# Gate and up of the first column group by turns, finer first splits, one place for split tiles in all phases, norm transposes apart

## The chip, the cores and the metric

The kernel runs on one core of one Trainium2 chip. The metric is the device time of one execution in microseconds (us). A core has a matrix engine (PE, with its weight loads PEld), a vector engine (DVE), a scalar engine (ACT), a third elementwise engine (POOL), and a queue engine that issues the weight loads from memory (SP). The granted clock of PE is written as a share of its full speed.

## The reference, cut to what matters

A decoder layer on x of 256 rows by 2048 columns, all in float32: a SwiGLU half-step (ffn1), a mixer of attention and gated linear attention, a cross-attention into 256 memory rows, and a second SwiGLU half-step (ffn2).

```python
def swiglu(h, w_gate, w_up, w_down):
    return (jax.nn.silu(h @ w_gate) * (h @ w_up)) @ w_down
...
        x = x + 0.5 * swiglu(rms_norm(x, ffn1_norm[l]), ffn1_w_gate[l], ffn1_w_up[l], ffn1_w_down[l])
        x = x + hybrid_mixer(rms_norm(x, mix_norm[l]), pos, w_in[l], attn_q_norm[l], attn_k_norm[l],
                             gla_w_gate2[l], gla_b_gate2[l], gla_out_norm[l], w_out[l])
        x = x + cross_attention(rms_norm(x, xattn_norm[l]), rms_norm(mem, mem_norm[l]),
                                xattn_w_q[l], xattn_w_k[l], xattn_w_v[l],
                                xattn_q_norm[l], xattn_k_norm[l], xattn_w_o[l])
        x = x + 0.5 * swiglu(rms_norm(x, ffn2_norm[l]), ffn2_w_gate[l], ffn2_w_up[l], ffn2_w_down[l])
```

w_gate and w_up have 2048 x 5632 elements, w_down 5632 x 2048.

## The kernel before, in words

**Precision and tiles.** Every float32 product is made of three passes in a reduced format: a weight tile `raw` of 1 MiB (128 partitions, four k-steps of 512 columns) is split into `wh` (a cast on ACT) and `wl = raw - wh` (a subtraction on DVE), both recorded at L145 in `split`, and PE adds wh·xh, wl·xh and wh·xl. One such tile against the 256 rows is a group of 24 matmuls of 512 columns. Activations stand transposed and split as xTh and xTl (a pair for each of four chunks of 512 columns), hTh and hTl, and sh and sl (sums for the Strassen products).

**Phases.** `open_phase` and `close_phase` stack a pool for the half-step phases (half1, half2) and for the middle phase between. `wh` and `wl` have three places each in a half-step, four smaller ones in the middle phase; raw tiles come from `wp` (three places) and in a half-step, by turns, from the phase's own three (`load`, L130 and below). `in_turn` keeps the weight loads, the casts and the subtractions each in the program's order.

**A half-step** (`ffn`, L372 and below) takes 11 column groups of gate and up in the parts 0 to 3, 4 to 7, 8 to 10, and after each part the products with w_down. The first column group is a plain projection (`proj`): gate's four k-groups, then up's four. All others, and w_down, go through `strassen` (L228 and below): six products P1 to P6 of 12 matmuls each on two PSUM tiles x and y, then whole groups of 24 with one more product (on `ral`, with the sum accumulated by DMA) between. P1 takes the left tile `ral`; DVE then adds the right tile to it (L237), which is split again for P2, added to again and split again for P3. ACT evicts c0l (L254) and ys (L260), DVE makes c0r = ys - x (L264), which must be done before P5 writes x again, and c1r (L269). L219 and L184 are the matmuls in a Strassen, L175 to L177 those of a plain projection.

**Turning h and x.** h of a column group is transposed on PE (L383) two steps of the program after it is made (`later(2, ...)`, counted by `tick`), and hTh is copied by ACT (L302) and hTl subtracted by DVE (L303). At the end of ffn1 and at the end of the cross-attention `norm_chunk` squares a finished chunk of x on ACT (L332) and transposes it one step later (L343); DVE multiplies by the gain (xg, L345), ACT and DVE split (L348, L349).

**The order of work.** A scheduler puts each engine's instructions in a row by priority; `tc.high_priority(WPRI)` (200) lifts the splits of weights, evictions and accumulations. The split of h (L301 to L303) is not lifted. At the start, three raw tiles of gate and three tiles `xr` of x transposed are requested ahead of everything (L115 and below); `first` multiplies xr by the gain (POOL, or ACT for the first four pieces) and splits it. `load_x` fetches x in rows and squares it.

## Time and profile before

| what | value |
| --- | --- |
| median of three runs | 1917.93 us (1915.93 to 1919.88) |
| the profiled execution: its time | 1920.29 us |
| its span in the trace | 1918.5 us |
| PE busy | 1890.5 us, 99% |
| DVE busy | 1459.3 us, 76% |
| ACT busy | 1080.1 us, 56% |
| POOL busy | 125.7 us, 7% |
| mean granted clock | 0.995 |
| bytes moved by DMA | 453.90 MB, 237 GB/s in the mean |

A row of the timeline gives the start in us from the span's start, the busy time, the engine, the line of the kernel, the operation with what it writes and reads, the count of instructions put together in the row, and in square brackets the idle time of the engine ahead of it with what released it. Where several instructions stand in one row the busy time is that of all of them. The windows give busy time of each engine in a stretch, the mean granted clock, the share of the DMA engines and the bytes per second.

### The profile page before, as it was taken

How to read it: one execution, taken by the hardware profiler on the slowest of the kernel's cores; microseconds unless marked ns; L12 is line 12 of the kernel's file. 1: busy time of each engine (PE TensorE's matmuls, PEld its weight loads, DVE VectorE, ACT ScalarE, POOL GpSimd, SP SyncE). 2: the span in 40 equal slices, each digit the busy share in tenths (PEclk: the TensorE clock that was granted, in tenths of full speed). 3: DMA queues.
4: the chain of work that ended last, by engine and by line, in shares of the span. 5: the costliest groups of instructions: out<-in, count | busy, mean ns of one | idle time of the engine just before them, and what ended most of it. 6: DMA issues, size and time to landing. Idle time of an engine off the chain costs nothing.

```text
span 1918.5 us, 21566 instructions
## 1 busy us (share of the span) xinstructions
PE 1890.5 (99%) x8616; PEld 1563.4 (81%) x8616; DVE 1459.3 (76%) x1159; ACT 1080.1 (56%) x1028; POOL 125.7 (7%) x137
## 2 busy tenths in 40 slices
PE   8999999999999999999999999899999999999998
PEld 6888888888888778778888889788888888888876
DVE  7779887788888885446785555777888878888886
ACT  6556655555555556444676445555655556556553
POOL 2000000000000000002230000000000000000000
PEclk9999999999999999999999999899999999999999
DMA  9776787777877754445465554668768777787775
GB/s 376 274 244 225 241 301 280 275 240 241 277 246 274 250 157 174 169 158 194 174 221 200 195 193 157 254 198 293 231 230 285 259 275 272 246 284 233 242 253 171
DMA packets 68480, 453.90 MB, mean 237 GB/s; under 512 B 7675, under 2 KB 8827, under 8 KB 15004
## 3 DMA queue, kind: packets, MB, share of 16 engines
q1 hardware_dynamic: 56284, 370.74, 49.2%
q0 software_dynamic: 10944, 79.70, 18.5%
q10 hardware_dynamic: 1152, 2.10, 0.3%
q8 instruction: 67, 1.10, 0.2%
q14 instruction: 33, 0.27, 0.0%
HBM read 379.10 MB, written 6.29 MB: 201 GB/s over the span
## 4 chain that ended last, share of the span: by engine, by line
PE 93%; DVE 4%; issue 1%; ACT 1%; DMA 1%; POOL 0%; SPq 0%; DVEq 0%; POOLq 0%; ACTq 0%
PE acc L184 24%; PE x L219 17%; PE acc L176 9%; PE acc L177 9%; PE acc L175 9%; PE acc L219 9%; PE x L184 8%; PE y L219 4%; DVE wl L145 2%; ACT wh L145 1%; PE tp L383 1%; DVE raw L237 1%; DMA xr<-in_xT_dram 0%; DMA raw<-raw 0%; PE tp L343 0%
## 5 line engine op out<-in xcount | busy, mean ns | idle before, releaser
L145 DVE TENSOR_TENSOR wl<-raw,wh 128x2048 fp32r<-128x2048 f32 (+2 forms) x523 | 1013.6, 1954 | 367.1 <-ACT wh L145 366.7
L145 ACT CAST wh<-raw 128x2048 fp32r<-128x2048 f32 (+2 forms) x523 | 852.2, 1640 | 621.3 <-DVE raw L237 182.2
L175 PE MATMUL acc<-wh,xTh 128*128 128x512 f32 x544 | 216.3, 399 | 9.0 <-ACT wh L145 8.8
L176 PE MATMUL acc<-wl,xTh 128*128 128x512 f32 x544 | 214.9, 395 | 4.6 <-DVE wl L145 4.6
L177 PE MATMUL acc<-wh,xTl 128*128 128x512 f32 x544 | 214.2, 394 | 0.0
L237 DVE TENSOR_TENSOR raw<-raw 128x2048 f32<-128x2048 f32 x64 | 146.5, 2290 | 1.7
L241 POOL DMA_DIRECT2D raw<-raw x64 | 55.0, 860 | 1201.2 <-ACT sg L420 473.8
L175 PEld LDWEIGHTS acc<-wh,xTh 128*128 128x128 f32 x544 | 103.1, 190 | 32.4 <-ACT wh L145 10.5
L176 PEld LDWEIGHTS acc<-wl,xTh 128*128 128x128 f32 x544 | 103.6, 190 | 28.0 <-DVE wl L145 6.9
L184 PE MATMUL acc<-wl,xTh 128*128 128x512 f32 x480 | 121.8, 389 | 0.0
L184 PE MATMUL acc<-wh,xTl 128*128 128x512 f32 x480 | 121.8, 389 | 0.0
L184 PE MATMUL acc<-wh,xTh 128*128 128x512 f32 x480 | 121.8, 389 | 0.0
L177 PEld LDWEIGHTS acc<-wh,xTl 128*128 128x128 f32 x544 | 103.6, 190 | 21.7
L184 PEld LDWEIGHTS acc<-wl,xTh 128*128 128x128 f32 x480 | 90.1, 188 | 18.7
L184 PEld LDWEIGHTS acc<-wh,xTh 128*128 128x128 f32 x480 | 90.1, 188 | 18.7
L184 PEld LDWEIGHTS acc<-wh,xTl 128*128 128x128 f32 x480 | 90.1, 188 | 18.7
L219 PE MATMUL x<-wh,sh 128*128 128x512 f32 x256 | 71.2, 400 | 3.3 <-ACT wh L145 1.9
L219 PE MATMUL x<-wh,sl 128*128 128x512 f32 x256 | 68.8, 390 | 0.0
L219 PE MATMUL x<-wl,sh 128*128 128x512 f32 x256 | 68.7, 390 | 0.0
L420 ACT ACTIVATE sg<-acc,r 128x512 f32<-128x512 f32 x24 | 16.3, 689 | 84.7 <-PE acc L184 84.7
L184 PE MATMUL acc<-wh,hTl 128*128 128x512 f32 x232 | 59.2, 390 | 2.4 <-DVE hTl L303 2.4
L184 PE MATMUL acc<-wh,hTh 128*128 128x512 f32 x232 | 59.2, 390 | 0.9 <-ACT wh L145 0.9
(339 smaller groups left out, 2828.3 us busy)
## 6 DMA issues: line engine op xcount, KB each, us to landing
raw<-in_ffn_w_up_dram SPq DMA_DIRECT2D x88, 1024.0 KB, 8.9
raw<-in_ffn_w_down_dram SPq DMA_DIRECT2D x88, 1024.0 KB, 7.6
raw<-in_ffn_w_gate_dram SPq DMA_DIRECT2D x85, 1024.0 KB, 7.8
raw<-raw POOLq DMA_DIRECT2D x64, 1024.0 KB, 6.9
raw<-in_w_in_dram SPq DMA_DIRECT2D x48, 1024.0 KB, 4.8
raw<-in_w_out_dram SPq DMA_DIRECT2D x16, 1024.0 KB, 4.8
sl<-ffn_sl POOLq DMA_DIRECT2D x4, 1024.0 KB, 9.4
sh<-ffn_sh POOLq DMA_DIRECT2D x4, 1024.0 KB, 13.3
```

Source lines behind the costliest of these rows:

```text
L145: return SC.copy(wh, src), V.tensor_sub(wl, src, wh.bitcast(F32))
L175: PE.matmul(acc[t], lh, wh, start=first and i == 0, stop=False, skip_group_check=seeded)
L176: PE.matmul(acc[t], lh, wl, start=False, stop=False, skip_group_check=seeded)
L177: PE.matmul(acc[t], ll, wh, start=False, stop=last and i == len(half) - 1, skip_group_check=seeded)
L184: PE.matmul(acc[t], lhs(w[0], t)[i], w[1 + j], start=False, stop=last and j == 1 and n == len(group) - 1, skip_group_check=True)
L219: PE.matmul(acc, lhs(k)[i], w[:, k], start=first, stop=j == 1 and k == 3, skip_group_check=not start)
L237: V.tensor_add(dst, x, y)
L241: G.dma_start(dst, x, accum_op=ALU.add)
L383: PE.transpose(tp[:, j], hs[t][:, j * P:(j + 1) * P], ident)
L420: SC.activation(s, gate[t], AF.Silu, scale=r[:, t:t + 1])
```

## The change

Seven edits, none of which alters what is computed:

- `open_phase` reserves the places of wh and wl first, in every phase, then raw and h in a half-step, so that these lie in the same memory in all phases.
- The first three loads are gate's group 0, up's group 0 and gate's group 1, instead of gate's 0, 1, 2; only the first and third bring a tile of x.
- Raw tiles come three by three from `wp` and from the phase's pool, instead of by turns.
- The first column group goes through the new `plain_pair`: gate and up by turns, k-group after k-group, each tile split in two halves (the very first in four). The Strassen products of gate and up then take groups 2 and 3, and the whole groups are 0 and 1 (before: the other way round).
- The transposes of odd chunks in `norm_chunk` come three steps later instead of one.
- The split of h is lifted by WPRI.
- x in rows is requested in `first`, behind the tiles of x transposed for groups 2 and 3; its squares are lifted in `load_x`.

```diff
@@ -65,6 +65,15 @@
+        for tag in ("wh", "wl"):
+            if half_step:
+                FT(tag, FWB, [P, 4, 512], F32R, tag)
+            else:
+                FT(tag, WB, [P, 2, 512], F32R, tag)
+        if half_step:
+            FT("raw", FRAW, [P, 4, 512], F32, "raw")
+            FT("h", 8, [P, 4, S], F32, "h")
+
@@ -115,26 +124,30 @@
-        for g in range(3):
+        for i, (W, g) in enumerate((("gate", 0), ("up", 0), ("gate", 1))):
...
-            step = 2 if g else 1
-            xr = FT("h", 8, [P, 4, S], F32, "xr")
-            xload.append(xr)
+            step = 2 if i else 1
+            if i != 1:
+                xr = FT("h", 8, [P, 4, S], F32, "xr")
+                xload.append(xr)
             for k in range(0, 4, step):
-                SY.dma_start(xr[:, k:k + step], A["xT"][g, :, k:k + step])
-                SY.dma_start(raw[:, k:k + step], A["ffn1_w_gate"][0, g, :, k:k + step])
+                if i != 1:
+                    SY.dma_start(xr[:, k:k + step], A["xT"][g, :, k:k + step])
+                SY.dma_start(raw[:, k:k + step], A[f"ffn1_w_{W}"][0, g, :, k:k + step])
...
+            nth = phase["loads"]
             phase["loads"] += 1
-            if phase["half_step"] and phase["loads"] % 2:
+            if phase["half_step"] and nth % 6 >= 3:
@@ -148,7 +161,7 @@
-    def wgroup(W, c, g, fine=None):
+    def wgroup(W, c, g, fine=None, step=None):
...
-                for i in range(m if fine else 1):
-                    d = slice(i, i + 1) if fine else slice(0, m)
+                for i in range(0, m, step or m):
+                    d = slice(i, i + (step or m))
@@ -285,18 +298,29 @@
+    def plain_pair(Wl, cl, Wr, cr, lhs, groups, fine=None):
+
+        accs = tuple(tuple(pa.tile([P, 512], F32, tag="acc", name="acc") for _ in range(TT)) for _ in range(2))
+        for i, g in enumerate(groups):
+            for acc, W, c in zip(accs, (Wl, Wr), (cl, cr)):
+                own = fine if i == 0 and acc is accs[0] else None
+                for h, half in enumerate(wgroup(W, c, g, own, 1 if own else 2)):
+                    mm3(acc, lhs, half, i == 0 and h == 0, i == len(groups) - 1 and h == 1)
+                    tick()
+                if fine and acc is accs[0] and g < NC - 1:
+                    fine(4 * g + 4)
+        return accs
@@ -348,7 +372,7 @@
-        later(1, turn)
+        later(1 + 2 * (c % 2), turn)
@@ -382,7 +406,8 @@
-                split_from_psum(hi[:, :, sl], lo[:, :, sl], tp)
+                with tc.high_priority(WPRI):
+                    split_from_psum(hi[:, :, sl], lo[:, :, sl], tp)
@@ -407,30 +432,26 @@
-                    gate = proj(wg, f, lhs_x, range(4), fine)
+                    gate, upv = plain_pair(wg, f, wu, f, lhs_x, range(NC), fine)
+                    with tc.high_priority(120):
+                        sums = sums_of(xT[2], xT[3])
...
-                    gate, upv = strassen(wg, f, wu, f, lhs_x, (0, 1), sums, (2, 3),
+                    gate, upv = strassen(wg, f, wu, f, lhs_x, (2, 3), sums, (0, 1),
...
-                if plain:
-                    upv = proj(wu, f, lhs_x, range(4))
...
-                    with tc.high_priority(WPRI):
-                        sums = sums_of(xT[0], xT[1])
@@ -494,6 +515,9 @@
+                if k > 4:
+                    for c in (k // 2 - 4, k // 2 - 3):
+                        SY.dma_start(xs[c], A["x"][0, :, c * 512:(c + 1) * 512].rearrange("(t p) d -> p t d", p=P))
@@ -501,8 +525,7 @@
             with tc.high_priority(XPRI - 34 * c):
-                SY.dma_start(xs[c], A["x"][0, :, c * 512:(c + 1) * 512].rearrange("(t p) d -> p t d", p=P))
-            sumsq(c, xs[c], ss1)
+                sumsq(c, xs[c], ss1)
```

Three places of the order in which the engines take their instructions. In these rows a line number is that of the kernel that the row is from (L145 before is L158 after, L237 is L250, L264 is L277, L303 is L327, L332 is L356, L345 is L369, L348 is L372, L420 is L447), and a number behind a name tells one tile from another of that name.

ACT around the first Strassen of ffn1 (ral is raw_464 before and raw_481 after), before:

```order
L145 CAST wh_477<-raw_464 128x2048
L145 CAST wh_496<-raw_464 128x2048
L332 ACTIVATE junk_304,ss1_287<-x3_103 128x512
L332 ACTIVATE junk_306,ss1_287<-x3_103 128x512
L145 CAST wh_531<-raw_464 128x2048
L420 ACTIVATE sg_314<-acc_125,r1_312 128x512
L420 ACTIVATE sg_316<-acc_126,r1_312 128x512
L254 COPY acc_474<-x_472 128x512
L145 CAST wh_548<-raw_470 128x2048
L260 COPY ys_528<-y_473 128x512
```

And after:

```order
L158 CAST wh_400<-raw_398 128x1024 x2
L447 ACTIVATE sg_467<-acc_126,r1_465 128x512
L158 CAST wh_494<-raw_481 128x2048
L447 ACTIVATE sg_469<-acc_127,r1_465 128x512
L158 CAST wh_513<-raw_481 128x2048
L267 COPY acc_491<-x_489 128x512
L273 COPY ys_545<-y_490 128x512
L326 CAST hTh_529<-tp_531 128x4x128
L326 CAST hTh_529<-tp_538 128x4x128
L158 CAST wh_548<-raw_481 128x2048
```

The first sg (the SiLU of gate's columns) moved ahead of the first cast of ral, the second ahead of the next one, and the halves of the last plain tiles stand ahead of both.

DVE at the last Strassen of ffn1 (ral is raw_4548 before and raw_4565 after; xg are the chunks of x under the next norm), before:

```order
L145 TENSOR_TENSOR wl_4621<-raw_4548,wh_4620 128x2048
L237 TENSOR_TENSOR raw_4548<-raw_4548,raw_4552 128x2048
L345 TENSOR_TENSOR xg_4584<-tp_4579,gain_73 128x512
L345 TENSOR_TENSOR xg_4593<-tp_4588,gain_73 128x512
L345 TENSOR_TENSOR xg_4604<-tp_4599,gain_73 128x512
L345 TENSOR_TENSOR xg_4613<-tp_4608,gain_73 128x512
L145 TENSOR_TENSOR wl_4640<-raw_4548,wh_4639 128x2048
L145 TENSOR_TENSOR wl_4657<-raw_4554,wh_4656 128x2048
L264 TENSOR_TENSOR acc_4559<-ys_4636,x_4556 128x512
L145 TENSOR_TENSOR wl_4674<-raw_4550,wh_4673 128x2048
```

And after:

```order
L158 TENSOR_TENSOR wl_4637<-raw_4565,wh_4636 128x2048
L158 TENSOR_TENSOR wl_4674<-raw_4571,wh_4673 128x2048
L158 TENSOR_TENSOR wl_4691<-raw_4567,wh_4690 128x2048
L158 TENSOR_TENSOR wl_4708<-raw_4569,wh_4707 128x2048
L158 TENSOR_TENSOR wl_4726<-raw_4723,wh_4725 128x2048
L369 TENSOR_TENSOR xg_4601<-tp_4596,gain_73 128x512
L369 TENSOR_TENSOR xg_4610<-tp_4605,gain_73 128x512
L277 TENSOR_TENSOR acc_4576<-ys_4633,x_4573 128x512
L373 TENSOR_TENSOR xTl0_4595<-xg_4601,xTh0_4594 128x4x128
L373 TENSOR_TENSOR xTl0_4595<-xg_4610,xTh0_4594 128x4x128
L369 TENSOR_TENSOR xg_4659<-tp_4654,gain_73 128x512
```

Before, four xg stood ahead of the wl of P3 and the eviction of c0r (L264) behind two more wl. After, five wl stand in a row, then two xg, then the eviction (L277); the last of the five is that of the first whole group.

ACT at the entry of ffn2 (junk are the squares of x2 and x3 ahead of the norm; wh_9030 before and wh_9055 after are the first split of gate), before:

```order
L332 ACTIVATE junk_9006,ss4_8798<-x2_102 128x512
L332 ACTIVATE junk_9008,ss4_8798<-x2_102 128x512
L332 ACTIVATE junk_9012,ss4_8798<-x3_103 128x512
L332 ACTIVATE junk_9014,ss4_8798<-x3_103 128x512
L348 CAST xTh2_9046<-xg_9053 128x4x128
L145 CAST wh_9030<-raw_9028 128x2048
L348 CAST xTh2_9046<-xg_9062 128x4x128
L348 CAST xTh3_9066<-xg_9073 128x4x128
L145 CAST wh_9100<-raw_9098 128x2048
L145 CAST sh_9318<-fa_9320 128x1024
L145 CAST wh_9130<-raw_9128 128x2048
```

And after:

```order
L372 CAST xTh1_8987<-xg_9003 128x4x128
L356 ACTIVATE junk_9027,ss4_8817<-x2_103 128x512
L356 ACTIVATE junk_9031,ss4_8817<-x3_104 128x512
L158 CAST wh_9055<-raw_9053 128x1024 x2
L158 CAST wh_9107<-raw_9105 128x1024 x2
L158 CAST wh_9159<-raw_9157 128x1024 x2
L356 ACTIVATE junk_9033,ss4_8817<-x3_104 128x512
L158 CAST wh_9191<-raw_9189 128x1024 x2
L372 CAST xTh2_9073<-xg_9080 128x4x128
L372 CAST xTh2_9073<-xg_9089 128x4x128
```

The casts of the first three weight tiles moved ahead of the last square and of both xTh of chunk 2, each in two halves.

## Rows read from the trace of the kernel before

**Rows 1.** The page: the share of busy time of PE, and the engines' shares of the chain that ended last.

```profile
PE 1890.5 (99%) x8616; PEld 1563.4 (81%) x8616; DVE 1459.3 (76%) x1159; ACT 1080.1 (56%) x1028; POOL 125.7 (7%) x137
...
PE 93%; DVE 4%; issue 1%; ACT 1%; DMA 1%; POOL 0%; SPq 0%; DVEq 0%; POOLq 0%; ACTq 0%
```

**Rows 2.** Windows: the stretch, its length, then busy time (count) of PE, PEld, DVE, ACT and POOL, the granted clock, the DMA share and GB/s; the start, the steady part behind it, the end of ffn1, the entry of ffn2, the tail.

```profile
12.50:25.00 12.50, 6.50 (x17) 4.52 (x17) 8.91 (x7) 8.00 (x8) 8.18 (x6) 0.73 1.03 424
25.00:54.00 29.00, 29.00 (x129) 24.04 (x128) 23.00 (x17) 16.11 (x21) 3.28 (x3) 1.00 1.02 423
...
676.00:690.00 14.00, 12.09 (x54) 9.67 (x53) 11.98 (x10) 10.41 (x14) 0.88 (x2) 0.88 0.55 112
...
1212.00:1226.50 14.50, 8.48 (x30) 6.26 (x29) 14.50 (x18) 10.07 (x10) 2.02 (x2) 0.65 0.96 372
...
1876.00:1892.00 16.00, 13.96 (x60) 10.93 (x60) 13.59 (x9) 7.47 (x6) 1.33 (x2) 1.00 0.80 237
```

**Rows 3.** The timeline of the start, of PE, POOL, ACT and DVE.

```profile
12.56 0.40 PE L177 MATMUL acc<-wh,xTl 128*128 128x512 f32 x1
17.36 0.73 PE L175 MATMUL acc<-wh,xTh 128*128 128x512 f32 x2 [4.40 <-ACT wh L145]
...
25.25 0.39 PE L175 MATMUL acc<-wh,xTh 128*128 128x512 f32 x1
...
11.37 1.21 POOL L325 TENSOR_TENSOR xr<-xr,gain 128x512 f32<-128x512 f32 x1 [9.87 <-DMA xr<-in_xT_dram]
...
17.55 2.98 POOL L325 TENSOR_TENSOR xr<-xr,gain 128x512 f32<-128x512 f32 x1 [0.42 <-DMA xr<-in_xT_dram]
...
15.41 1.89 ACT L145 CAST wh<-raw 128x2048 fp32r<-128x2048 f32 x1
...
17.34 2.29 DVE L145 TENSOR_TENSOR wl<-raw,wh 128x2048 fp32r<-128x2048 f32 x1 [1.11 <-ACT wh L145]
```

**Rows 4.** The timeline of the first Strassen of ffn1: PE at P1 (59.93), P2, P3 and P5, and ACT's first and third cast of ral.

```profile
59.93 1.07 PE L219 MATMUL x<-wh,xTh 128*128 128x512 f32 x4
...
62.65 1.07 PE L219 MATMUL y<-wh,sh 128*128 128x512 f32 x4
...
66.20 1.20 PE L219 MATMUL x<-wh,sh 128*128 128x512 f32 x4 [0.67 <-ACT acc L254]
...
72.69 0.61 PE L219 MATMUL x<-wh,sh 128*128 128x512 f32 x2
...
49.25 1.91 ACT L145 CAST wh<-raw 128x2048 fp32r<-128x2048 f32 x1 [2.25 <-PE acc L177]
...
62.60 1.91 ACT L145 CAST wh<-raw 128x2048 fp32r<-128x2048 f32 x1 [3.52 <-DVE r1t L363]
```

**Rows 5.** The timeline of the end of ffn1, of PE and DVE; 676.02 is P1 of the last Strassen.

```profile
662.27 2.12 PE L184 MATMUL acc<-wh,hTh 128*128 128x512 f32 x8 [0.34 <-ACT wh L145]
665.89 1.19 PE L184 MATMUL acc<-wh,hTl 128*128 128x512 f32 x4 [1.50 <-DVE hTl L303]
...
676.02 1.07 PE L219 MATMUL x<-wh,hTh 128*128 128x512 f32 x4
...
682.09 0.66 PE L343 MATMUL tp<-ident,x 128*128 128x128 f32 x4 [1.88 <-DVE xg L345]
...
658.55 6.69 DVE L145 TENSOR_TENSOR wl<-raw,wh 128x2048 fp32r<-128x2048 f32 x3
```

**Rows 6.** The timeline of the entry of ffn2, of PE, ACT and DVE; the last row of ACT and the last of DVE split a sum of 128x1024.

```profile
1211.60 1.91 PE L343 MATMUL tp<-ident,x 128*128 128x128 f32 x16
1216.80 1.22 PE L175 MATMUL acc<-wh,xTh 128*128 128x512 f32 x2 [3.29 <-ACT wh L145]
...
1226.46 0.43 PE L175 MATMUL acc<-wh,xTh 128*128 128x512 f32 x1
...
1211.22 0.63 ACT L332 ACTIVATE junk<-x 128x512 f32<-128x512 f32 x1 [0.64 <-DVE x L985]
...
1214.85 1.90 ACT L145 CAST wh<-raw 128x2048 fp32r<-128x2048 f32 x1
...
1221.38 1.05 ACT L145 CAST sh<-fa 128x1024 fp32r<-128x1024 f32 x1 [0.43 <-DVE fa L207]
...
1218.41 2.28 DVE L145 TENSOR_TENSOR wl<-raw,wh 128x2048 fp32r<-128x2048 f32 x1
...
1224.62 1.21 DVE L145 TENSOR_TENSOR sl<-fa,sh 128x1024 fp32r<-128x1024 f32 x1
```

**Rows 7.** The timeline of the tail, of PE: a whole group of the last Strassen but one (1865.47, 1872.41), and P3 of the last (1888.96).

```profile
1865.47 1.07 PE L184 MATMUL acc<-wh,hTh 128*128 128x512 f32 x4
...
1872.41 1.08 PE L184 MATMUL x<-wh,hTl 128*128 128x512 f32 x4
...
1888.96 1.19 PE L219 MATMUL x<-wh,sh 128*128 128x512 f32 x4 [1.86 <-ACT wh L145]
```

**Rows 8.** The timeline of a Strassen of gate and up in the steady part of ffn2: the eviction of c0r and one hTl on DVE, both hTh on ACT, P5 on PE.

```profile
1774.40 0.69 DVE L264 TENSOR_TENSOR acc<-ys,x 128x512 f32<-128x512 f32 x1
1775.00 0.68 DVE L303 TENSOR_TENSOR hTl<-tp,hTh 128x512 fp32r<-128x512 f32 x1
...
1776.24 1.07 PE L219 MATMUL x<-wh,sh 128*128 128x512 f32 x4
...
1772.26 1.08 ACT L302 CAST hTh<-tp 128x512 fp32r<-128x512 f32 x2
```

More of the change, by code (lines that the diff above doesn't have):

```diff
@@ L132, in load @@
         if wload:
+            phase["loads"] += 1
             return wload.pop(0)
@@ L286, in strassen, with proj @@
         return accs
-    def proj(W, c, lhs, groups, fine=None):
+    def proj(W, c, lhs, groups):
         n = W.shape[-1]
@@ L293, in proj @@
         for i, g in enumerate(groups):
-            if fine and i:
-                fine(4 * i)
-            for h, half in enumerate(wgroup(W, c, g, fine if i == 0 else None)):
+            for h, half in enumerate(wgroup(W, c, g)):
                 mm3(acc, lhs, half, i == 0 and h == 0, i == len(groups) - 1 and h == 1)
@@ L413, in ffn @@
                 else:
-                    gate, upv = strassen(wg, f, wu, f, lhs_x, (0, 1), sums, (2, 3),
+                    gate, upv = strassen(wg, f, wu, f, lhs_x, (2, 3), sums, (0, 1),
                                          mid=sums_h if f == part[-1] else None)
-                sg = []
+                sg, hs = [], []
                 with tc.high_priority(WPRI):
@@ L421, in ffn @@
                         sg.append(s)
-                if plain:
-                    upv = proj(wu, f, lhs_x, range(4))
-                hs = []
-                with tc.high_priority(WPRI):
                     for t in range(TT):
@@ L431, in ffn @@
                 if plain:
-                    with tc.high_priority(WPRI):
-                        sums = sums_of(xT[0], xT[1])
                     kept = [tc.dram_tile([P, 2, 4, S], F32, name=f"{pre}_{n}") for n in ("sh", "sl")]
```

## The prediction

> **What bounds the kernel now.** I read the page's busy shares first, then the chain that ended last [rows 1]: PE is busy for 1890.5 of 1918.5 us, and 93% of the chain is PE. So only three things can move the time: fewer PE instructions, a higher clock, or fewer holes in PE. The change leaves the number of 512-column matmuls as it is, so I looked for the holes, in PE's timeline, then asked the windows what else was busy in each [rows 2]. PE's full pace is seen in product P1 of the first Strassen: 12 matmuls from 59.93 to 62.65 [rows 4], 2.72 us, 0.227 us each. Against that pace four places lose time that the change touches:
>
> - The start. From the matmul at 12.56 to the one at 25.25 PE issues 16, 3.6 us of work, in 12.7 us [rows 3]: 9.1 us lost. The second raw tile's cast starts at 15.41, its subtraction at 17.34. DMA is saturated (424 GB/s), and the granted clock is 0.73 in that window, a mix of the two levels [rows 2].
> - The end of ffn1: waits of 0.34, 1.50 (hTl, behind three wl) and 1.88 us (xg) [rows 5], 3.7 together; a clock of 0.88 over 14 us [rows 2], 1.7; and some 0.9 of slow pick-up behind the waits: 6.3.
> - The entry of ffn2. The transposes end at about 1213.5 (1211.60 and 1.91); at 1226.46 PE has done 15 matmuls since, 3.4 us of work in 13.0 [rows 6]: 9.6 lost, at a granted clock of 0.65 [rows 2].
> - The tail: from 1865.47 to 1888.96, 23.49 us, PE does 84 matmuls [rows 7], 19.05 us: 4.4 lost at full clock [rows 2].
>
> **The change, part by part.** Sums are made against the profiled run, 1920.29 us, which is 2.4 above the median of the three runs; what I take off, I take off the median too.
>
> A, the start. Up's first tile now stands where gate's second stood, and needs no new xT, so bytes before the second tile fall by half a MiB, and it comes in halves: casts of 1.05 and subtractions of 1.21 us for 128x1024 [rows 6], in place of 1.89 and 2.29 [rows 3]. Before, POOL starts on pieces at 11.37 and 17.55 [rows 3], at 1.75 and 4.0 MiB of the queue's order: 2.75 us a MiB; between 25 and 54 us at 423 GB/s [rows 2] it is 2.5. So up's first half (2.0 MiB) is there at about 12.1, cast at 13.2, subtracted at 14.4; the second half at 13.4, 14.5 and 15.7. PE comes free at 12.95 (12.56 and 0.39): it waits about 0.9. Gate's second tile, in halves with its xT, is ready at about 18, and PE is busy until 19.3. One later wait of 0.4 (gate's third tile, ACT behind the squares) I keep. So P1 of the first Strassen starts at about 52.4 instead of 59.93 [rows 4]: 7.5 gained so far.
>
> F, the first Strassen, takes part of that back. It needs a chain of cast, subtraction, addition, cast, subtraction, addition, cast on ral: from the cast at 49.25 to the end of the one at 62.60, 15.3 us [rows 4]. In the new order ACT has the first sg ahead of that first cast, and sg waits for gate's last group. That ends one group of 24 matmuls (5.4 us) before P1, at 47.0, so the chain starts at about 47.6 and ends at 62.9; PE with eight transposes between wants P3 at 58.6. P3 then starts at about 63.1 against 66.20, and P5 at about 68.7 against 72.69 [rows 4]. A and F together: 4.0. Ends: 7.5 if ACT gets to the cast before sg; 0 if the clock falls in the 4.5 us of waits (below) and POOL costs 2 us more.
>
> POOL is the cost that the trace only brackets: the same multiplication of xr took 1.21 us at 11.37 and 2.98 at 17.55, as DVE ran 2.29 us of subtraction [rows 3]. The new order puts subtractions earlier, beside the multiplications. Two at 2.98 instead of 1.2 would bring gate's second half to about 21.4, when PE wants it at 22.0: hidden, just; later ones may show 2 us, which is in the range. The Trainium skill, "GPSIMD Engine Reference", section 1 (Specifications), says that this engine's SBUF interfaces are shared with VectorE and that it contends with its instructions of two SBUF inputs; a subtraction is one, so by that page every multiplication here goes at the slow price, which I take as the bound only: the row at 11.37 ran without such a neighbour.
>
> B, the end of ffn1. The split of hT is now of high priority, so both hTl come ahead of the Strassen eviction and the 1.50 goes; the transposes of the two chunks stand apart, so the 1.88 goes. P1 of the last Strassen can start at about 673.6 instead of about 676. But DVE then carries five wl in a row (2.29 us each) ahead of xg and the eviction of c0r, and PE has the first whole group, which needs the fifth wl, ahead of P5. Counted through by the durations of the rows: PE waits 1.0 for P3's weights, 1.0 for that group's wh, 2.8 for its wl, 0.3 for the eviction, with pick-up 5.3. Gain 6.3 - 5.3 = 1.0, between -2 (clock falls again) and 4 (wl come in the order PE needs).
>
> C, the entry of ffn2. Before, the first cast (1214.85) stands on ACT behind an xTh of the third chunk, and the first wl starts at 1218.41, behind sums and gains [rows 6]. Now the casts of three half-split tiles stand directly behind the first square of x3, the one at 1211.22: half a tile is cast by about 1213.0 and its wl there by 1214.2, while the transposes fill PE to 1213.5. I keep 0.4 for the wl and 0.7 for pick-up: 1.1 lost instead of 9.9 (9.6 and the rest to full pace). Gain 8.8; 3 if the first split still waits for places of the middle phase.
>
> D, the tail. The same hTl change. Before, PE took eight matmuls of the other group first; the slot of wh came free when x<-wh,hTl ended (1872.41 and 1.08), and from there the chain of ral set P3 [rows 7]. With hTl in time that slot is free about 4.3 earlier; two hTl earlier on DVE (1.3) may cost 0.8 of it. Gain 3.5 to 4.3: 4.0; 2.5 as the low end.
>
> E, the other Strassens. hTl always goes ahead of the eviction of c0r. Where both now stand before it, it ends at about 1775.1 + 1.2 = 1776.3 by the rows, and P5 wants it at 1776.24 [rows 8]. So about 0.07 us in each of the eleven Strassens where the order newly has both ahead: -0.8. It could be 0 or -10 (0.5 us in twenty). The spaced transposes elsewhere, the raw tiles three by three and x's loads behind xT I cost at nothing: DMA has 1 MiB to bring per 5.4 us of matmuls in the steady part and the window at 25 to 54 us shows no hole in PE (29.00 of 29.00) [rows 2].
>
> Sum: 4.0 + 1.0 + 8.8 + 4.0 - 0.8 = 17.0. The clock: after the wait of 1.88 it fell (0.88 in that window), after 1.86 in the tail it did not (1.00) [rows 2, 5, 7]. So a wait of 2 to 3 us is a coin's throw, and there are two such places, F (2.5 us at stake) and B (1.7): I take off 2.0, about one of them. The Trainium skill, "TensorE: Matmul & The Clock Gate", section "What's actually happening", says that the slow clock is the default and that activity lifts it; the tail's row shows that one wait of this length need not bring it back, so the page alone settles neither place. 17.0 - 2.0 = 15.0: **1917.93 - 15.0 = 1903**.
>
> **The rivals.**
> - Given back: both clock falls (-4.2 instead of -2.0), POOL's 2 us in sight, B at -1. 17.0 - 2.0 - 4.2 - 2.0 = 8.8: 1909. For it: DVE is already the late engine in all four places.
> - The shared places bind: the first wl of ffn2 still waits for the middle phase, C is 3 instead of 8.8: 15.0 - 5.8 = 9.2, also 1909. For it: tiles that share places wait for the last reader in the old phase. Against it: w_o's last reader is done at 1211.6, before the new cast.
> - No stall in F (ACT's queue is not bound by sg) and B at 4: 15.0 + 3.5 + 2.0 + 3.0 = 23.5: 1894.
> - Slower: the eviction of c0r. Its price is what two hTl of 0.69 us cost when the transposes come late: DVE stands at the first hTl, and P5 with it. It decides from 0.8 us in each of the 20 Strassens of gate and up, and at 1.0 gives 15.0 + 0.8 - 20 x 1.0 = -4.2, so 1922. For it: the slack at 1776.24 is nil. Against it: ACT has both hTh done by 1773.34 in the steady rows, before the three wl there end at 1774.40 [rows 8], so that DVE would seldom have to stand.
>
> **How the numbers follow.** Forecast 0.52; given back 0.18; shared places 0.08; no stall 0.10; slower 0.08; something that nets to nothing 0.04. Forecast, the three rivals below 1914 and their spread lie between 1893 (26.8 at most: 7.5 + 4 + 9.9 + 4.4 and no E, is 1892) and 1912; about 2 in 10 stay out. Within 0.2% (3.8 us, about what a measurement of this kernel can tell from no change) are 1914.1 to 1921.8: 0.07 with the ends of the first two rivals. Faster 0.86, slower 0.07.
>
> **What would show it.** In the profile after: the hole at 12.95 shrinks to 1 us; the first Strassen starts near 52 and PE waits before its P3 some 4 us; the 1.50 for hTl is gone at 666 and in the tail, and PE waits for a wl before P5 of ffn1's last Strassen; PE's first matmul of ffn2 follows its transposes with no more than 1 us, at full clock. I am wrong if PE waits in every Strassen for the eviction of c0r, or if PE's work itself grows.

## The result, and the profile after

| kernel | median, us | runs | ratio to the kernel before, 95% interval |
| --- | --- | --- | --- |
| before | 1918.58 | 4 | 1 |
| after | 1904.80 (1904.26 to 1907.18) | 4 | 0.9932 (0.9915 to 0.9950) |
| predicted | 1903 (1893 to 1912) | | |

The change takes off 13.8 us; 15.0 were forecast. The profiled execution of the changed kernel took 1907.18 us (span 1905.4), 13.1 less than that of the kernel before.

PE's work is what it was. From the profile's page, the busy time of each engine, then their shares of the chain that ended last:

```profile
PE 1885.5 (99%) x8616; PEld 1558.4 (82%) x8616; DVE 1462.5 (77%) x1174; ACT 1080.9 (57%) x1043; POOL 123.6 (6%) x137
...
PE 86%; DMA 6%; DVE 4%; ACT 2%; issue 1%; SPq 0%; POOL 0%; ACTq 0%; DVEq 0%; POOLq 0%
```

The same 8616 instructions of PE, 5 us less busy (fewer of them at the lower clock), and now 6% of the chain in DMA, which had 1% [rows 1]. To see every hole I added up, over each stretch of the trace, by how much the distance between the starts of two PE instructions exceeds the median distance for their shape. That is the time PE loses; the stretches are cut at fixed times.

| stretch (us from the span's start) | before | after | three by three only at first (second run) | all three mends |
| --- | --- | --- | --- | --- |
| 0 to 56: start | 13.1 | 6.5 | 5.7 | 6.7 |
| 56 to 80: first Strassen | 1.0 | 5.0 | 4.9 | 2.4 |
| 80 to 635: ffn1 | 0.4 | 2.2 | -0.1 | -0.4 |
| 635 to 708: end of ffn1 | 7.1 | 3.7 | 5.3 | 1.5 |
| 708 to 1190: middle | 12.1 | 12.5 | 11.6 | 11.5 |
| 1190 to 1228: entry of ffn2 | 10.1 | 0.6 | 0.6 | 0.6 |
| 1228 to 1828: ffn2 | 0.4 | 4.0 | 0.6 | 0.2 |
| from 1828: tail | 5.4 | 1.6 | 1.5 | 2.3 |

The last two columns are experiments (below). Now the rows of after that answer to [rows 2 to 8].

Windows (columns as in [rows 2]) of the start, the first Strassen, the end of ffn1 and the entry of ffn2:

```profile
12.50:25.00 12.50, 12.01 (x53) 9.57 (x52) 12.09 (x9) 7.52 (x10) 6.43 (x4) 1.00 1.03 419
...
56.00:70.00 14.00, 11.22 (x45) 8.68 (x45) 12.03 (x8) 9.95 (x9) 0.88 (x1) 0.88 0.63 140
670.00:690.00 20.00, 17.01 (x78) 13.31 (x77) 17.66 (x11) 13.26 (x15) 1.12 (x2) 1.00 0.84 222
...
1208.00:1225.00 17.00, 16.90 (x81) 13.79 (x79) 16.83 (x22) 12.25 (x16) 1.07 (x1) 1.00 0.96 399
```

PE is all but full at the start and at the entry of ffn2, with a granted clock of 1.00. The clock's only fall while PE works is in the first Strassen (0.88); at the end of ffn1 it stayed up (1.00).

The timeline of the start, of PE, ACT, DVE and POOL (compare [rows 3]):

```profile
12.93 0.63 PE L188 MATMUL acc<-wh,xTh 128*128 128x512 f32 x2
14.05 0.51 PE L189 MATMUL acc<-wl,xTh 128*128 128x512 f32 x1 [0.49 <-DVE wl L158]
...
11.70 1.05 ACT L158 CAST wh<-raw 128x1024 fp32r<-128x1024 f32 x1 [0.58 <-DMA raw<-in_ffn_w_up_dram]
...
12.77 3.21 DVE L158 TENSOR_TENSOR wl<-raw,wh 128x1024 fp32r<-128x1024 f32 x2 [0.94 <-ACT wh L158]
...
13.79 1.11 POOL L349 TENSOR_TENSOR xr<-xr,gain 128x512 f32<-128x512 f32 x1 [12.29 <-DMA xr<-in_xT_dram]
...
20.54 3.98 POOL L349 TENSOR_TENSOR xr<-xr,gain 128x512 f32<-128x512 f32 x2 [3.66 <-DMA xr<-in_xT_dram]
```

Up's first half is cast at 11.70 (forecast: there at 12.1), and PE's wait of 4.40 has become 0.49.

The first Strassen (compare [rows 4]), PE at P1 and P3, and ACT from the first sg on:

```profile
53.27 1.07 PE L232 MATMUL x<-wh,xTh 128*128 128x512 f32 x4
...
62.90 1.39 PE L232 MATMUL x<-wh,sh 128*128 128x512 f32 x4 [2.69 <-ACT wh L158]
...
46.73 0.69 ACT L447 ACTIVATE sg<-acc,r 128x512 f32<-128x512 f32 x1 [1.73 <-PE acc L190]
47.31 1.90 ACT L158 CAST wh<-raw 128x2048 fp32r<-128x2048 f32 x1
...
53.95 1.91 ACT L158 CAST wh<-raw 128x2048 fp32r<-128x2048 f32 x1 [4.16 <-DVE raw L250]
...
59.97 1.08 ACT L326 CAST hTh<-tp 128x512 fp32r<-128x512 f32 x2
60.92 7.32 ACT L158 CAST wh<-raw 128x2048 fp32r<-128x2048 f32 x4
```

The chain of ral starts at 47.31 behind sg (forecast 47.6), and P3 at 62.90 (forecast 63.1). P1 came at 53.27, 0.9 later than forecast, so PE's wait before P3 was 2.69 us and not some 4.

The end of ffn1 (compare [rows 5]), PE at the first whole group of the last Strassen, and DVE:

```profile
685.28 1.20 PE L197 MATMUL acc<-wh,hTh 128*128 128x512 f32 x4 [1.20 <-ACT wh L158]
...
689.19 0.96 PE L197 MATMUL acc<-wl,hTh 128*128 128x512 f32 x3 [1.79 <-DVE wl L158]
...
678.03 11.10 DVE L158 TENSOR_TENSOR wl<-raw,wh 128x2048 fp32r<-128x2048 f32 x5 [1.43 <-ACT wh L158]
```

The waits for hTl and xg are gone; DVE's five subtractions in a row and the two waits at the whole group are there, 3.0 us in place of the 3.8 forecast for the two.

The entry of ffn2 (compare [rows 6]):

```profile
1209.10 0.71 PE L188 MATMUL acc<-wh,xTh 128*128 128x512 f32 x2
...
1207.67 5.78 ACT L158 CAST wh<-raw 128x1024 fp32r<-128x1024 f32 x6
...
1208.73 6.90 DVE L158 TENSOR_TENSOR wl<-raw,wh 128x1024 fp32r<-128x1024 f32 x6
...
1225.39 1.22 DVE L217 TENSOR_TENSOR fa<-xTh,xTl 128x1024 f32<-128x1024 f32 x1
```

PE goes from its transposes into the first product without a wait that the view names. The last row is the first of the sums for the Strassen products. Before the change DVE made it ahead of the first subtraction (1218.41 in [rows 6]):

```profile
1212.41 1.22 DVE L204 TENSOR_TENSOR fa<-xTh,xTl 128x1024 f32<-128x1024 f32 x1
```

What was not forecast stands at the places where gate and up begin anew after w_down, four of them (near 277, 527, 1468 and 1724 us). The first, ACT, DVE and PE, and the queue of weight loads ahead of it:

```profile
234.67 8.13 SPq L154 DMA_DIRECT2D raw<-in_ffn_w_down_dram  x2
...
273.24 1.91 ACT L158 CAST wh<-raw 128x2048 fp32r<-128x2048 f32 x1 [1.97 <-DMA raw<-raw]
275.05 0.58 ACT L273 COPY ys<-y 128x512 f32<-128x512 f32 x1
...
277.39 0.69 DVE L277 TENSOR_TENSOR acc<-ys,x 128x512 f32<-128x512 f32 x1
...
278.13 1.20 PE L232 MATMUL x<-wh,sh 128*128 128x512 f32 x4 [1.08 <-DVE acc L277]
```

and the same place in the kernel before:

```profile
240.49 0.81 SPq L141 DMA_DIRECT2D raw<-in_ffn_w_down_dram  x2
...
274.82 1.92 ACT L145 CAST wh<-raw 128x2048 fp32r<-128x2048 f32 x1 [0.79 <-DMA raw<-raw]
```

P1 of that Strassen starts at 265.94 after and 268.97 before. The cast of rar, which waits for the accumulating transfer, starts 7.3 us behind P1 instead of 5.9, and ys, the eviction of c0r and P5 stand in a row behind it. Earlier, the two loads of w_down's last tiles go out 8 us apart instead of at once, the second 23.5 us ahead of P1 instead of 28.1; the later loads are queued behind it.

### The profile page after: what moved, and what is told of

Read it like the earlier page. It is cut to its first block, busy times and chain, and to the rows that moved or that the text cites. A ratio compares the mean times of both kernels' runs of the same rounds, so it can differ in the third digit from the quotient of the medians.

```text
span 1905.4 us, 21602 instructions
## 1 busy us (share of the span) xinstructions
PE 1885.5 (99%) x8616; PEld 1558.4 (82%) x8616; DVE 1462.5 (77%) x1174; ACT 1080.9 (57%) x1043; POOL 123.6 (6%) x137
## 4 chain that ended last, share of the span: by engine, by line
PE 86%; DMA 6%; DVE 4%; ACT 2%; issue 1%; SPq 0%; POOL 0%; ACTq 0%; DVEq 0%; POOLq 0%
PE acc L197 21%; PE x L232 15%; PE acc L189 9%; PE acc L190 9%; PE acc L188 9%; PE acc L232 8%; PE x L197 7%; PE y L232 3%; DMA raw<-in_ffn_w_gate_dram 3%; DVE wl L158 3%; DMA raw<-raw 3%; ACT wh L158 2%; DVE raw L250 1%; PE tp L407 1%; DMA xr<-in_xT_dram 1%
## 5 line engine op out<-in xcount | busy, mean ns | idle before, releaser
L158 DVE TENSOR_TENSOR wl<-raw,wh 128x2048 fp32r<-128x2048 f32 (+2 forms) x538 | 1016.0, 1908 | 358.7 <-ACT wh L158 357.6
L158 ACT CAST wh<-raw 128x2048 fp32r<-128x2048 f32 (+2 forms) x538 | 852.3, 1600 | 603.3 <-DVE raw L250 182.8
L250 DVE TENSOR_TENSOR raw<-raw 128x2048 f32<-128x2048 f32 x64 | 146.6, 2290 | 1.8
L447 ACT ACTIVATE sg<-acc,r 128x512 f32<-128x512 f32 x24 | 16.5, 690 | 90.1 <-PE acc L197 88.4
L197 PE MATMUL acc<-wl,hTh 128*128 128x512 f32 x232 | 59.3, 390 | 1.8 <-DVE wl L158 1.8
L232 PEld LDWEIGHTS x<-wh,sh 128*128 128x128 f32 x256 | 45.0, 188 | 19.5 <-DVE acc L277 4.5
```

What stands on the lines that cost most here:

```text
L158: return SC.copy(wh, src), V.tensor_sub(wl, src, wh.bitcast(F32))
L197: PE.matmul(acc[t], lhs(w[0], t)[i], w[1 + j], start=False, stop=last and j == 1 and n == len(group) - 1, skip_group_check=True)
L232: PE.matmul(acc, lhs(k)[i], w[:, k], start=first, stop=j == 1 and k == 3, skip_group_check=not start)
L250: V.tensor_add(dst, x, y)
L447: SC.activation(s, gate[t], AF.Silu, scale=r[:, t:t + 1])
```

## The experiments

All are variants of the changed kernel, and the diffs are against it unless another is named. A control of the changed kernel ran beside the first three; the later ones are compared with it too, as the kernel before took much the same beside all of them (1919.5, 1919.6 and 1919.3 us). A ratio's interval is some 2.5 us to either side, so differences of 1 to 3 us between variants are read together with the lost time in the traces.

**Control.**

> The changed kernel once more, unaltered, so that the variants beside it can be compared with it on the same chip. All theories: 0.993 of the kernel before, about 1905 us; in executions in which the clock falls in the first Strassen some 2 us more.

Measured: 1906.39 us, ratio 0.9934 (0.9921 to 0.9946). It is the base for what follows.

**Raw tiles by turns from the seventh load on.**

```diff
-            if phase["half_step"] and nth % 6 >= 3:
+            if phase["half_step"] and (nth >= 3 if nth < 6 else nth % 2):
```

> The changed kernel, with raw tiles three by three for the first six loads of a half-step only, and by turns from then on as before the change. In the changed kernel's trace PE waits in four places where gate and up begin anew after w_down (near 277, 527, 1468 and 1724 us, 5.2 us together); the accumulating transfer lands there 7.2 us after P1's start instead of 5.8, the cast of rar waits for it, ys stands behind that cast on ACT, and the eviction of c0r behind ys. Theory 1 (places): three by three gives ral's place, the last to come free, to an earlier load, so that up to four loads queue behind it and the memory queue is still full when the accumulating transfer is issued. Then by turns brings all four waits back to the 0.4 us of before: 5 us less than the changed kernel beside it, about 1900. Theory 2 (the lifted split of h): the waits are DVE's and ACT's order, and stay: the same as the changed kernel, within 1 us.

Measured: 1900.25 us, 0.9902 (0.9888 to 0.9915), and when run again as a base 1900.79 us, 0.9900 (0.9884 to 0.9916): 6.1 us less than the control. All four waits are gone (table above: 2.2 and 4.0 become -0.1 and 0.6). The rows at the first place, in the second run of it, with P1 at 265.12:

```profile
236.64 0.81 SPq L154 DMA_DIRECT2D raw<-in_ffn_w_down_dram  x2
...
271.24 1.92 ACT L158 CAST wh<-raw 128x2048 fp32r<-128x2048 f32 x1 [1.06 <-DMA raw<-raw]
...
265.12 1.07 PE L232 MATMUL x<-wh,xTh 128*128 128x512 f32 x4
```

The two loads go out at once again, some 28 us ahead of P1, and the cast starts 6.1 us behind it. Theory 1 holds: the three-by-three rule costs some 6 us once the phase runs. That it is ral's place which the second load waits for is read from the times at which subtractions end and loads go out, and was not tried by itself.

**sg behind the first cast of ral.** sg, h and the transposes of the first column group are recorded behind P1 of the next Strassen:

```diff
+        if waiting:
+            waiting.pop(0)(issued["cast"], 1)
...
+                            if cast:
+                                tc.add_manual_dep(ins.ins, cast, ...)
```

> The changed kernel, with sg and h of the first column group recorded behind P1 of the Strassen that follows, and sg held behind the first cast of ral on ACT. In the changed kernel's trace that cast starts at 47.31, behind sg, and PE waits 2.8 us before P3 (near 60 us), after which the clock is at its lower level for some 3 us in the profiled execution. Theory 1 (the prediction's step F): the chain of ral is what P3 waits for and sg is what its first cast waits for; ACT is done with the plain casts at 45.0 and ral has landed at 40.6, so the chain starts about 2 us earlier: 2 us less than the changed kernel where the clock did not fall in either, 3 to 4 less where it fell. Theory 2: the cast waits for a place of wh or for DVE anyway, and the wait stays: within 0.5 us of the changed kernel.

Measured: 1906.59 us, 0.9934 (0.9920 to 0.9947): nothing, the size of theory 2 but not for its reason. The first cast did start earlier, and the second stood at 50.79 instead of the control's 52.83, but the chain was held up further on. DVE and ACT there:

```profile
55.49 2.29 DVE L251 TENSOR_TENSOR raw<-raw 128x2048 f32<-128x2048 f32 x1
...
58.37 1.08 ACT L329 CAST hTh<-tp 128x512 fp32r<-128x512 f32 x2
59.32 7.43 ACT L159 CAST wh<-raw 128x2048 fp32r<-128x2048 f32 x4
```

The addition ends at 57.8; the third cast waits until 59.3, behind two hTh that this change lifted. sg alone is not the hinge.

**ys ahead of the cast of rar, everywhere.**

```diff
-        product(x, s_(2), parts(rar), False)
+        product(x, s_(2), parts(rar, ysc), False)
```

> The changed kernel, with the copy of ys always ahead of the cast of rar on ACT. Theory 1: at three of the four places (277, 527, 1724 us) P5 waits only because ys stands behind a cast that waits for a transfer; with ys ahead the eviction of c0r is early and these three waits, 3.4 us, go, though the transfer lands as late as ever: 3 us less than the changed kernel, unless the new order costs elsewhere. Theory 2: P5 then waits for rar's own cast or subtraction: within 1 us.

Measured: 1907.40 us, 0.9939 (0.9926 to 0.9951), 1 us more than the control. At the first of the places:

```profile
270.53 0.59 ACT L276 COPY ys<-y 128x512 f32<-128x512 f32 x1 [0.48 <-PE y L235]
...
273.67 2.29 DVE L158 TENSOR_TENSOR wl<-raw,wh 128x2048 fp32r<-128x2048 f32 x1 [1.39 <-ACT wh L158]
275.88 0.69 DVE L280 TENSOR_TENSOR acc<-ys,x 128x512 f32<-128x512 f32 x1
```

ys is 2.9 us earlier than in the control (273.42), and the eviction is not (275.75 there), since on DVE it stands behind rar's subtraction, which waits for the same transfer. Theory 1 falls: the row that a wait stood behind was one of two. The end of ffn1, however, lost 1.5 us instead of 4.1; that was used below. What it won there went elsewhere: the profiled execution, the slowest of the five, lost 8.6 us in ffn2, the control's 3.7, with a wait of 2.55 us before a P3 at 1718.67 that the control does not have.

**The split of hT not lifted.**

```diff
-                with tc.high_priority(WPRI):
-                    split_from_psum(hi[:, :, sl], lo[:, :, sl], tp)
+                split_from_psum(hi[:, :, sl], lo[:, :, sl], tp)
```

> The changed kernel, with the split of hT recorded at its ordinary priority as before the change. Theory 1 (steps B and D of the prediction): hTl falls behind the subtractions of the weights again, at the end of ffn1 the wait for hTl of about 1.5 us is back, and in the tail P3 of the last Strassen starts some 4 us later: 5 us more than the changed kernel, about 1911; the eviction of c0r goes ahead of hTl again, which gives back at most 0.5 us. Rival: hTl was late only through the transposes and weights of the old order, and nothing returns: within 1 us of the changed kernel.

Measured: 1911.16 us, 0.9957 (0.9943 to 0.9970), 4.8 more than the control. PE in the tail, then at the end of ffn1:

```profile
1861.25 1.20 PE L197 MATMUL acc<-wh,hTl 128*128 128x512 f32 x4 [1.35 <-DVE hTl L327]
1878.83 1.72 PE L232 MATMUL x<-wh,sh 128*128 128x512 f32 x4 [1.85 <-ACT wh L158]
...
664.71 1.19 PE L197 MATMUL acc<-wh,hTl 128*128 128x512 f32 x4 [1.36 <-DVE hTl L327]
```

and a window of the tail:

```profile
1876.00:1890.00 14.00, 12.14 (x47) 9.59 (x46) 11.54 (x8) 11.39 (x7) 0.84 (x1) 0.88 0.59 130
```

The tail loses 6.5 us instead of 2.0, as forecast, but some 1.7 of the 4.5 is a fall of the clock (0.88 over 14 us) behind the wait of 1.85, which the kernel before did not have there. At the end of ffn1 the wait for hTl is back and the waits at the whole group shrink by as much: 3.7 lost, against 4.1. The four waits after w_down stay (1.0, 0.9, 1.4, 1.1), so the lifted split is not their cause, and theory 1 holds.

**Norm transposes together.**

```diff
-        later(1 + 2 * (c % 2), turn)
+        later(1, turn)
```

> The changed kernel, with the norm transposes of both chunks of a pair one step later, as before the change. Theory 1: at the end of ffn1 PE stands in the fourth row of transposes for xg once more (1.88 us before), perhaps with a fall of the clock (1.7), and the two waits of the changed kernel there (1.4 and 2.0 us) go or stay with the order of the weights: between 0 and 3 us more than the changed kernel. Rival: the transposes apart are what puts the first whole group ahead of P5 and DVE's five subtractions in a row; together again, PE loses less there than the 3.4 us of the changed kernel: 1 to 2 us less.

Measured: 1912.77 us, 0.9965 (0.9952 to 0.9977), 6.4 more than the control. PE at the end of ffn1:

```profile
686.84 1.09 PE L367 MATMUL tp<-ident,x 128*128 128x128 f32 x4 [4.11 <-DVE xg L369]
```

With the other edits in place, PE stands 4.1 us for xg, twice as long as before the change [rows 5]: xg now comes behind four subtractions. The transposes apart are worth 6 us here, more than either theory said; the end of ffn1 loses 9.8 us instead of 4.1, of which some 1.7 is a fall of the clock (0.88 from 680 to 694 us).

**No shared places.** The reservation in `open_phase` is left out.

> The changed kernel, without the places reserved at the start of each phase. Theory 1 (places): the first weight splits of ffn2 lie again where tiles of the middle phase lay, wait for their last readers, and part of the 9.2 us that the changed kernel saves near 1212 us is lost: 4 to 9 us more, seen as a wait of ACT's or DVE's first split there. Rival: the order on ACT and DVE (casts ahead of the last square and of xTh) and the halves do it alone: within 1 us of the changed kernel.

Measured: 1906.88 us, 0.9936 (0.9924 to 0.9949), and the entry of ffn2 loses 0.6 us as in the control. The rival holds in its size: the places do nothing that can be measured. That the order and the halves do it is taken up below.

**Whole splits** in the first column group.

```diff
-                for h, half in enumerate(wgroup(W, c, g, own, 1 if own else 2)):
+                for h, half in enumerate(wgroup(W, c, g, own, 1 if own else None)):
```

> The changed kernel, with each tile of the first column group split whole (the very first still in four). Theory 1: at the start the second tile's cast waits for the whole tile (landing at 13.4 instead of 12.1) and takes 1.9 instead of 1.05 us, its subtraction 2.3 instead of 1.2: 2 to 3 us more there; at the entry of ffn2 cast and subtraction of the first tile end some 2 us later: 2 us more. Together 4 to 5 us more than the changed kernel. Rival: the order by turns and the places carry it, and PE has other work meanwhile: 1 to 2 us more.

Measured: 1909.52 us, 0.9949 (0.9936 to 0.9961), 3.1 more than the control. PE at the start, at P3 of the first Strassen, and at the entry of ffn2:

```profile
15.19 0.73 PE L188 MATMUL acc<-wh,xTh 128*128 128x512 f32 x2 [1.20 <-ACT wh L158]
...
63.39 1.19 PE L232 MATMUL x<-wh,sh 128*128 128x512 f32 x4 [0.24 <-ACT wh L158]
...
1211.15 0.73 PE L188 MATMUL acc<-wh,xTh 128*128 128x512 f32 x2 [1.07 <-ACT wh L158]
```

The start loses 9.9 us instead of 5.4, and the first Strassen 1.1 instead of 5.0. P3 is at 63.39, 1.6 us behind the control's 61.76, and the clock falls at the start (0.88 from 12 to 26 us) instead of behind P3 (1.00 from 56 to 70, the control 0.88). So of the 4.5 us that the halves win at the start all but 0.6 is handed back by the end of the first Strassen; at the entry of ffn2 they win 1.4. The sum lies between the theory and the rival.

**Gate, then up**, with the first loads of before:

```diff
-        for i, (W, g) in enumerate((("gate", 0), ("up", 0), ("gate", 1))):
+        for i, (W, g) in enumerate((("gate", 0), ("gate", 1), ("gate", 2))):
...
-        for i, g in enumerate(groups):
-            for acc, W, c in zip(accs, (Wl, Wr), (cl, cr)):
+        for acc, W, c in zip(accs, (Wl, Wr), (cl, cr)):
+            for i, g in enumerate(groups):
```

> The changed kernel, with gate's four groups first and then up's, and gate's groups 0, 1 and 2 as the first loads, each with its tile of x, as before the change; the halves and all else stay. Theory 1 (steps A and F): the start loses 3 to 4 us more, as each second tile brings half a MiB of x, but sg is made 20 us earlier and the chain of ral is ready for P3, so that the 4 us lost in the first Strassen go: within 1.5 us of the changed kernel. Rival: the chain is late for another reason (its transfers), the first Strassen loses 4 us as ever, and the kernel is 3 to 4 us slower than the changed one.

Measured: 1908.66 us, 0.9946 (0.9933 to 0.9959), 2.3 more than the control. PE at the start, and at P3 of the first Strassen, which does not wait:

```profile
13.72 0.73 PE L186 MATMUL acc<-wh,xTh 128*128 128x512 f32 x2 [1.29 <-ACT wh L156]
...
64.54 1.17 PE L230 MATMUL x<-wh,sh 128*128 128x512 f32 x4
```

The start loses 11.4 us, 6.0 more than the control's 5.4, and the first Strassen 0.5 instead of 5.0; here too the clock falls at the start (0.88 from 12 to 26 us) and not in the first Strassen (1.00). The second half of theory 1 holds, its first was too small, so the sum lies between theory and rival.

**Two more mends on top of the by-turns kernel.**

> The changed kernel with raw tiles three by three for the first six loads only, once more, as the base for the two kernels that build on it: 0.990 of the kernel before, about 1900 us.

The first holds sg behind the first cast of ral, and the two hTh of the first column group behind the third cast too (the diff is against the kernel with sg alone):

```diff
-            waiting.pop(0)(issued["cast"], 1)
+            waiting.pop(0)(issued["cast"], 2)
...
+        ins = SC.copy(hi, ps)
+        if cast:
+            tc.add_manual_dep(ins.ins, cast, ...)
```

> That base, with sg behind the first cast of ral as in the earlier run, and now also both hTh of the first column group behind the third cast of ral, where the trace of the earlier run showed that cast standing behind them (59.32, though the addition had ended at 57.8). Theory 1: with nothing else ahead, the chain of ral ends near 59.7 and PE, which wants P3 at about 58.6, waits 1 us instead of 2.8; the clock then need not fall: 2 to 4 us less than the base. Theory 2: DVE's two h, which wait for up's sums on PE, or a place of wh hold the chain: within 1 us.

Measured: 1898.08 us, 0.9891 (0.9876 to 0.9907), 2.7 less than its base, as theory 1 said, though P3 still waits 1.60 us. The slowest execution is 0.7 us above the fastest of the base; in the traces the first Strassen loses 2.4 us instead of 4.9. The clock stays at 1.00 in that window:

```profile
60.48 1.20 PE L233 MATMUL x<-wh,sh 128*128 128x512 f32 x4 [1.60 <-ACT wh L159]
...
56.00:70.00 14.00, 12.18 (x57) 9.63 (x56) 11.40 (x8) 10.70 (x8) 0.88 (x1) 1.00 0.69 144
```

The second puts ys ahead of rar's cast too, only in the two Strassens on w_down at the end of ffn1 (`ahead`; the diff is against the kernel before this one):

```diff
-                                mid=sums_back if c and not end else None, last=last and end and c == NC - 2)
+                                mid=sums_back if c and not end else None, last=last and end and c == NC - 2, ahead=end and not last)
```

> The same, and in the last Strassen pair of ffn1 (under the next norm) the copy of ys ahead of the cast of rar. Where that was done everywhere, the end of ffn1 lost 1.5 us instead of 4.1, because the scheduler then put the eviction of c0r and P5 ahead of the first whole group and of its fifth subtraction. Theory 1 (the prediction's step B: five subtractions in a row): the waits of 1.4 and 2.0 us there go, 2 to 3 us less than the kernel without it. Rival: the order of the rest moves too and new waits of that size come: within 1 us.

Measured: 1894.41 us (1893.93 to 1895.47), 0.9871 (0.9857 to 0.9885): 3.7 less than without it, 12 less than the control, and 24.9 less than the kernel before. DVE at the end of ffn1, with a window in which PE is busy for 33.94 of 34 us:

```profile
673.02 4.50 DVE L159 TENSOR_TENSOR wl<-raw,wh 128x2048 fp32r<-128x2048 f32 x2 [1.43 <-ACT wh L159]
677.43 1.28 DVE L378 TENSOR_TENSOR xg<-tp,gain 128x512 f32<-128x512 f32 x2
678.63 0.69 DVE L283 TENSOR_TENSOR acc<-ys,x 128x512 f32<-128x512 f32 x1
...
656.00:690.00 34.00, 33.94 (x158) 27.68 (x157) 31.08 (x23) 22.58 (x23) 1.74 (x2) 1.00 0.79 251
```

Two subtractions instead of five stand ahead of xg and the eviction, and the end of ffn1 loses 1.5 us instead of 5.4: theory 1.

## Why the prediction held, step by step

The sum came out close to the forecast (13.8 and 15.0 us), but two of its terms, B and E, were off by 2.4 and 4.6 us in opposite directions. That they half cancelled is luck. In lost time of the two profiled executions (13.9 us by the steps, of the 13.1 between them; the middle and the end of the span take the rest):

- **A and F, start and first Strassen**: 14.1 before, 11.5 after, a gain of 2.6; forecast 4.0, less about 2.0 for a fall of the clock here or at the end of ffn1. Right, with its mechanism: the chain started at 47.31, P3 at 62.90, and the clock fell in the window. The whole-splits and the gate-then-up kernels show the coupling from the other side: of what the start loses more there (4.5 and 6.0 us), 3.9 and 4.5 come back in the first Strassen, some 1.7 of it the clock. sg was the first hold-up of several.
- **B, end of ffn1**: 7.1 to 3.7, a gain of 3.4 against 1.0. Two of the four waits came where they were put, 3.0 us at the whole group instead of 3.8; P3 and P5 did not wait, and the clock stayed up.
- **C, entry of ffn2**: 10.1 to 0.6, 9.5 against 8.8. The rival of the shared places is void: without them the gain is the same. Which edit makes the gain is shown only in part. Of those undone one by one, the halves give back 1.4 us, the transposes together 0.6, the others nothing. Two were never undone there: the sums of xT, which are now made behind the first column group (DVE's first stood at 1212.41, ahead of the first subtraction; now at 1225.39, behind those of the first four tiles), and the first six loads three by three. The list of the change does not name the first; its diff does. That the bulk of the 9.5 us is the order that comes of it is read from these rows, and not shown by a run.
- **D, tail**: 5.4 to 1.6, 3.8 against 4.0. When the split is not lifted 4.5 go, some 1.7 of them a fall of the clock; so 2.8 of the gain are shown to be the split's, and that step is right.
- **E, the other Strassens**: 0.8 lost before, 6.2 after, 5.4 more where 0.8 was forecast. This term was the most mis-sized, and its mechanism was another. Step E laid it to hTl ahead of the eviction of c0r, and said that the raw tiles three by three cost nothing, as DMA has 1 MiB to bring per 5.4 us of matmuls in the steady part. That step failed. By turns again, with the split still lifted, the loss is 0.5: so hTl ahead of the eviction costs nothing that can be measured, and the rule of three by three costs the 5.4. Its price is not in the bytes, which are the same. It falls due only where w_down ends and gate and up begin, where a load goes out late and the accumulating transfer then lands late. That this load waits for the place that comes free last is read from the trace and not shown by itself. The rival of the slower side named the right instruction, c0r before P5, for the wrong reason.

Two slips in the prediction change nothing: the most that it adds up (7.5 + 4 + 9.9 + 4.4) is 25.8 and not 26.8, and its 1892 comes from 25.8; and the multiplication at 11.37 was not quite without a neighbour, as DVE ran a subtraction of 0.69 us from 10.99 on.

The contention of POOL and DVE shows at the start, on both engines. Two subtractions of 128x1024 took 3.21 us from 12.77 on, where one alone takes 1.21 [rows 6], so the one beside POOL's multiplication took 2.0; that multiplication took 1.11, and two later ones 3.98 together. PE's wait there was 0.49, and the 2 us kept in the range were not needed. The long times come out near what standing until the other engine ends would give (by an estimate from these rows the second subtraction would end at 14.90 + 1.21 = 16.1, and ended at 15.98); no run tried it. The Trainium skill, "GPSIMD Engine Reference", section 1 (Specifications), names contention with VectorE instructions of two SBUF inputs; the rows agree that it is there, and show that it does not slow every multiplication.

## What to carry to other kernels

- Where the bound engine is 99% busy, list its holes by place and price each; the sum of places is a forecast. But also ask of each edit "without a price" what it does where phases meet, not in the steady part: a rule of places that leaves the bytes as they are cost 6 us there.
- Work won ahead of a chain that is longer than what covers it is handed back at the chain's end. Shorten the chain, instruction by instruction on each engine that it passes, before winning more ahead of it.
- A wait named by one engine's row can stand behind two rows. Undoing one and finding nothing (sg, ys) means that the next one is looked for, not that the chain is innocent.

## What the runs showed that was not expected

Waits of about the same length did or did not bring the clock down. 2.69 us before P3 did (0.88 in 56 to 70 us), 1.20 and 1.79 us within 4 us at the end of ffn1 did not (1.00 in 670 to 690 us), and 1.60 us before P3 in the mended kernel did not. Even the same wait at the same product went either way: P3 of the last Strassen waited 1.86 us before the change and the clock stayed at 1.00 [rows 2, 7], and 1.85 us with the split not lifted, and it fell to 0.88 over 14 us. The four executions of the changed kernel had mean granted clocks of 0.999, 0.999, 1.000 and 1.000, the control's five 0.998 to 0.999; one fall of 1.7 us makes about 0.001, so by that estimate it came in seven of nine. A stall of some 2 us on PE is therefore uncertain by the 1.7 us of a fall. That is less than the interval of the ratios here (some 2.5 to 3.3 us to either side), so a single fall is seen in the trace and not in the medians.
